# Splitting the second half of x before the first evictions of the value product

## The chip, the cores and the metric

The kernel runs on one core of one Trainium2 chip. The metric is the device time of one execution in microseconds (us), taken as the median of several runs. Everything below about the chip is read from one profiled execution.

## The reference

The kernel computes one layer of a decoder trunk for 1024 tokens of width 1024, in float32. Only the first lines matter here.

```python
h = x @ w_in                       # columns = [pool | q | k | v | forget-gate]
pool_out = pool_mixer(u, pool_w, pool_scale)
attn_out = forgetting_attention(q, k, v, f_logit)     # 8 heads, causal
x = layer_norm(alpha * x + concat(pool_out, attn_out) @ w_out)
x = layer_norm(alpha * x + relu(x @ w_mlp1)**2 @ w_mlp2)
```

The stage that the change touches is the part of `x @ w_in` that gives the values v and the forget-gate logits, 520 columns together.

## The kernel before

**Split products.** A float32 operand is held as a high part and a low part. `split(hi, lo, src)` makes them with one cast on ScalarE (hi, L71) and one subtraction on VectorE (lo, L72, which reads hi). A product of two such operands is three matmuls into the same PSUM bank: hi by hi (L83), hi by lo (L84), lo by hi (L85), in the helper `three`.

**The value product.** Tokens come in two halves of 512 (c = 0 and 1), each as four blocks of 512 KB that `load_x(c, kp)` loads into a staging slot (tag "Q") and splits into slots of tag "B", two k-tiles of 128 rows for each block. The weights `wvf` come in four blocks of 520 KB. For the first half eight PSUM banks, all that there are, are accumulated at once: 4 token tiles by 2 column halves (260 columns each), with the contraction index k outermost, so 8 x 8 x 3 = 192 matmuls. `vf_out` then evicts each bank: a ScalarE cast (L161), a VectorE subtraction (L162) and a small VectorE addition that takes the gate logits (L164). After that the second half runs bank by bank, again 192 matmuls. Its matmuls need two things: the splits of x for c = 1, and a bank that `vf_out` has released.

**Output weights.** Between the tiles of the second half, `split_output_weights(k)` splits five 512 KB blocks of `wout` (ScalarE cast L198, VectorE subtraction L199), and GpSimd stores both parts to DRAM (L201, ten stores of 512 KB). These blocks are loaded behind x on the SyncE queue (L194), and three 512 KB blocks of the next weights `wuqk` (L76, tag "S") follow them. What comes next on TensorE is the first pool projection, `pool_group`, with its own weights.

**Order of work.** The kernel is traced in the order of its source, and a planner then fixes the order of the instructions on each engine before the program runs: among those that it takes to be ready it prefers the one traced first, and slots of one tag are given out in the order in which they were asked for. So the order on an engine need not be the order of the source. On the chip each engine follows the order given and waits on semaphores. `tc.issue_after(ins)` adds for every instruction traced in its block an edge that places it behind `ins` on the engine of `ins`; instructions of other engines get none, and no semaphore is added.

Of the kernel before, what the change touches and what calls it, by code (L numbers as in the profile page):

```python
# [8 lines left out]
F32 = mybir.dt.float32  # L9
# [3 lines left out]
ALU = mybir.AluOpType  # L13
# [23 lines left out]
def trunk(ctx, tc, xT, xn, wuqk, wvf, bf, poolw, pscale, wout, g1, b1, w1, w2, g2, b2, out):  # L37
# [5 lines left out]
    nc = tc.nc  # L43
# [7 lines left out]
    def slot(tag, shape, dt=F32R):  # L51
        uid[0] += 1
        return sb.tile([P] + list(shape), dt, tag=tag, bufs=NBUF[tag], name=f"{tag}{uid[0]}")
# [9 lines left out]
    def bank(tag=None):  # L63
        uid[0] += 1
        if tag is None:
            tag = CYCLE[rr[0] % 8]
            rr[0] += 1
        return ps.tile([P, CH], F32, tag=tag, bufs=PBUF[tag], name=f"{tag}{uid[0]}")

    def split(hi, lo, src):  # L70
        nc.scalar.copy(hi, src)  # L71
        nc.vector.tensor_tensor(lo, src, hi.bitcast(F32), ALU.subtract)  # L72

    def load_w(src):
        st = slot("S", [KT, P], F32)
        nc.sync.dma_start(st, src)  # L76
        w = slot("B", [2, KT, P])
        split(w[:, 0], w[:, 1], st)
        return w[:, 0], w[:, 1]
# [35 lines left out]
    def load_x(c, kp):  # L115
        st = slot("Q", [2, CH], F32)
        x = slot("B", [2, 2, CH])
        if c or kp:
            nc.sync.dma_start(st, xT[c, kp])
        for k in range(2):  # L120
            t = x[:, k]
            xs[c, 2 * kp + k] = t
            first = c == kp == k == 0
            for i, r in enumerate((slice(0, 256), slice(256, CH)) if first else (slice(0, CH),)):
                if c == kp == 0:
                    (nc.scalar if first and i == 0 else nc.sync).dma_start(st[:, k, r], xT[c, kp, :, k, r])
                split(t[:, 0, r], t[:, 1, r], st[:, k, r])
                yield

    wv = []  # L130

    def load_wvf(kp):
        st = slot("S", [2, 2 * VW], F32)
        hi, lo = slot("A", [2, 2 * VW]), slot("A", [2, 2 * VW])
        wv.append((hi, lo))
        if kp:
            nc.sync.dma_start(st, wvf[kp])
        for k in range(2):
            if kp == 0:
                nc.sync.dma_start(st[:, k], wvf[kp, :, k])  # L140
            for c in [slice(0, VW), slice(VW, 2 * VW)] if kp == 0 and k == 0 else [slice(0, 2 * VW)]:
                split(hi[:, k, c], lo[:, k, c], st[:, k, c])
                yield
# [4 lines left out]
    def vf_mm(t, half, dst, k):  # L148
        x = xs[t // 4, k]
        tok = slice((t % 4) * P, (t % 4 + 1) * P)  # L150
        cols = slice(half * VW, (half + 1) * VW)
        w = wv[k // 2]
        three(dst, (x[:, 0, tok], x[:, 1, tok]), (w[0][:, k % 2, cols], w[1][:, k % 2, cols]), k == 0, k == KT - 1)

    def vf_out(t, half, src):
        if V[t] is None:
            v2 = slot("B", [2, NH, 2, HD])
            V[t - t % 2], V[t - t % 2 + 1] = v2[:, 0], v2[:, 1]
        vv = V[t][:, 4 * half : 4 * half + 4]
        sv = src[:, 0 : 4 * HD].rearrange("p (h d) -> p h d", h=4)  # L160
        nc.scalar.copy(vv[:, :, 0, :], sv)  # L161
        nc.vector.tensor_tensor(vv[:, :, 1, :], sv, vv[:, :, 0, :].bitcast(F32), ALU.subtract)  # L162
        hs = slice(4 * half, 4 * half + 4)
        nc.vector.tensor_tensor(z[:, t, hs], src[:, 4 * HD : VW], bf_sb[:, hs], ALU.add)  # L164


    acc0 = [tuple(bank()[:, 0:VW] for _ in range(2)) for t in range(4)]
# [5 lines left out]
    for kp in range(4):  # L173

        gw, gx = load_wvf(kp), load_x(0, kp)
        for g in (gw, gx, gw, gx, gw, gx):
            next(g, None)
    nc.sync.dma_start(bf_sb, bf)
    nc.sync.dma_start(ps_sb, pscale)
    for k in range(KT):  # L180
        for t in range(4):
            for half in range(2):
                vf_mm(t, half, acc0[t][half], k)
    for t in range(4):
        for half in range(2):
            vf_out(t, half, acc0[t][half])
    for kp in range(4):
        for _ in load_x(1, kp):
            pass

    raw = {}
    for k in range(ASIDE, KT):
# [10 lines left out]
    for t in range(4, NT):  # L203
        for half in range(2):
# [4 lines left out]
            k = ASIDE + 2 * (t - 4) + half  # L209
# [1049 lines left out]
```

## Time and profile before

| | |
|---|---|
| Median of 3 runs | 1039.18 us (1038.84 to 1039.32) |
| The profiled execution, its time | 1040.64 us |
| The profiled execution, its span from first to last instruction | 1038.9 us |
| Mean granted TensorE clock | 0.996 of full speed |
| TensorE busy | 1018.5 us, 98% of the span |
| VectorE / ScalarE / GpSimd busy | 756.6 / 513.6 / 155.0 us |

The span leaves out 1.74 us of the execution's own time that lie around it. The engines are named PE (TensorE matmul), PEld (its weight load), DVE (VectorE), ACT (ScalarE), POOL (GpSimd) and SP (SyncE); a q behind a name is the engine's queue that issues transfers.

### The profile page before, as it was taken

The numbers are of one execution on the slowest core, as the hardware profiler recorded it, in microseconds if no ns is written. First come the engines' busy times: TensorE is split into PE (matmuls) and PEld (weight loads), VectorE is DVE, ScalarE is ACT, GpSimd is POOL, SyncE is SP. The second block draws the span as 40 slices with busy tenths as digits, with TensorE's granted clock in tenths as the row PEclk, the third lists the DMA queues.
The fourth block names the chain that finished last, engine by engine and source line by source line (L and its number), as shares of the span: only waits on it lengthen the run. The fifth ranks groups of instructions, "written<-read, shape, count | busy, mean of one in ns | idle before, by whom it ended". The sixth has DMA issues, their size and how long they took to land.

```text
span 1038.9 us, 14121 instructions
## 1 busy us (share of the span) xinstructions
PE 1018.5 (98%) x4976; PEld 846.5 (81%) x4976; DVE 756.6 (73%) x1300; ACT 513.6 (49%) x823; POOL 155.0 (15%) x267
## 2 busy tenths in 40 slices
PE   9999999999989999999999999999999999999996
PEld 9988887888767888787888888888878888888884
DVE  4777678677767887989888778788885666565547
ACT  4523566666665332676666766768621211122152
POOL 0200112112100031112122122120100000000047
PEclk9999999999999999999999999999999999999998
DMA  9702311111584532139767567565999888878753
GB/s 359 273 28 82 111 65 32 36 47 54 173 281 140 185 122 99 61 125 353 275 229 276 224 253 273 217 265 184 346 316 321 283 258 283 275 222 269 242 186 121
DMA packets 113671, 206.30 MB, mean 199 GB/s; under 512 B 9592, under 2 KB 78008, under 8 KB 113600
## 3 DMA queue, kind: packets, MB, share of 16 engines
q1 hardware_dynamic: 94608, 137.63, 40.5%
q0 software_dynamic: 18560, 67.12, 16.7%
q8 instruction: 39, 0.64, 0.2%
q10 hardware_dynamic: 432, 0.66, 0.2%
q14 instruction: 32, 0.26, 0.1%
HBM read 132.42 MB, written 72.94 MB: 198 GB/s over the span
## 4 chain that ended last, share of the span: by engine, by line
PE 49%; issue 4%; DVE 3%; DMA 2%; POOL 1%; ACT 0%; DVEq 0%; POOLq 0%; SPq 0%
PE s L1060 15%; PE pv L1060 8%; PE s L727 8%; PE mm L727 6%; PE pt L727 6%; PE pv L727 4%; PE pt L1060 2%; PE mm L1060 2%; DMA S<-in_w_dram 2%; DVE B L72 1%; DMA hid_dram<-A 1%; POOL hid_dram L852 0%; POOL A L720 0%; DVE A L850 0%; DVE bns L573 0%
## 5 line engine op out<-in xcount | busy, mean ns | idle before, releaser
L71 ACT CAST B<-S 128x1024 fp32r<-128x1024 f32 (+1 forms) x78 | 67.7, 881 | 169.4 <-DMA S<-in_w_dram 67.5
L727 PE MATMUL s<-B,Q 128*128 128x512 f32 x492 | 116.4, 389 | 0.2 <-ACT B L71 0.2
L727 PEld LDWEIGHTS s<-B,Q 128*128 128x128 f32 x492 | 92.3, 188 | 19.8 <-ACT B L71 0.6
L72 DVE TENSOR_TENSOR B<-S,B 128x1024 fp32r<-128x1024 f32 (+1 forms) x78 | 78.0, 1008 | 34.0 <-ACT B L71 33.9
L1060 PE MATMUL s<-B,Q 128*128 128x512 f32 x402 | 98.2, 390 | 0.0
L1060 PEld LDWEIGHTS s<-B,Q 128*128 128x128 f32 x402 | 75.5, 188 | 16.2
L71 ACT CAST Q<-S 128x1024 fp32r<-128x1024 f32 x53 | 55.7, 1051 | 58.0 <-PE s L727 17.0
L852 POOL DMA_DIRECT2D hid_dram<-A x90 | 48.1, 537 | 221.5 <-ACT A L849 164.6
L1060 PE MATMUL s<-B,A 128*128 128x512 f32 x321 | 79.7, 393 | 0.0
L72 DVE TENSOR_TENSOR Q<-S,Q 128x1024 fp32r<-128x1024 f32 x53 | 65.6, 1238 | 15.3 <-ACT Q L71 14.8
L727 PE MATMUL pt<-B,Q 128*128 128x512 f32 x312 | 74.6, 389 | 0.0
L727 PE MATMUL mm<-B,Q 128*128 128x512 f32 x300 | 71.6, 389 | 0.0
L1060 PEld LDWEIGHTS s<-B,A 128*128 128x128 f32 x321 | 60.3, 188 | 13.5
L727 PEld LDWEIGHTS pt<-B,Q 128*128 128x128 f32 x312 | 58.5, 188 | 12.1
L727 PEld LDWEIGHTS mm<-B,Q 128*128 128x128 f32 x300 | 56.3, 188 | 11.7
L377 ACT ACTIVATE A<-A,nm 128x1024 f32<-128x1024 f32 (+7 forms) x64 | 49.7, 778 | 32.3 <-DVE nm L375 31.1
L416 PE MATMUL pv<-A,B 128*128 128x256 f32 x320 | 62.2, 295 | 2.7 <-DVE A L399 1.3
L416 PEld LDWEIGHTS pv<-A,B 128*128 128x128 f32 x320 | 51.0, 188 | 17.1 <-ACT A L398 6.9
L399 DVE TENSOR_TENSOR A<-pt,A 128x512 fp32r<-128x512 f32 (+1 forms) x80 | 49.6, 634 | 15.2 <-ACT A L398 14.4
L850 DVE TENSOR_TENSOR A<-A,A 128x1024 f32<-128x1024 f32 x45 | 53.6, 1219 | 0.0
L362 POOL TENSOR_TENSOR A<-A,maskb 128x128 f32<-128x128 f32 x48 | 23.5, 492 | 190.8 <-DVE nm L375 131.8
L398 ACT CAST A<-pt 128x512 fp32r<-128x512 f32 (+1 forms) x80 | 41.4, 542 | 19.3 <-PE pt L397 18.4
(427 smaller groups left out, 2341.7 us busy)
## 6 DMA issues: line engine op xcount, KB each, us to landing
hid_dram<-A POOLq DMA_DIRECT2D x105, 512.0 KB, 4.0
S<-in_w_dram SPq DMA_DIRECT2D x62, 512.0 KB
Q<-hid_dram SPq DMA_DIRECT2D x98, 256.0 KB
A<-hid_dram SPq DMA_DIRECT2D x82, 256.0 KB
S<-in_wuqk_dram SPq DMA_DIRECT2D x12, 512.0 KB
wo_dram<-Q POOLq DMA_DIRECT2D x10, 512.0 KB, 3.8
B<-wo_dram SPq DMA_DIRECT2D x10, 512.0 KB
Q<-hid_dram SPq DMA_DIRECT2D x39, 128.0 KB
```

The lines of the kernel that those rows point to most:

```text
L71: nc.scalar.copy(hi, src)
L72: nc.vector.tensor_tensor(lo, src, hi.bitcast(F32), ALU.subtract)
L362: nc.gpsimd.tensor_tensor(nb[:, qs], nb[:, qs], maskb, ALU.add)
L377: nc.scalar.activation(pt[:, :nk], pt[:, :nk], AF.Exp, bias=nm, scale=-1.0, accum_out=rsum[h][:, i : i + 1])
L398: nc.scalar.copy(tt[:, 0, ev], tp[:, ev])
L399: nc.vector.tensor_tensor(tt[:, 1, ev], tp[:, ev], tt[:, 0, ev].bitcast(F32), ALU.subtract)
L416: nc.tensor.matmul(ov, V[j][:, h].rearrange("p s d -> p (s d)"), tt[:, s, a:b], start=(j == 0 and s == 0), stop=(j == 2 * m + 1 and s == 1),)
L727: nc.tensor.matmul(dst, b[x][:, k], A[a][y][:, k], start=first and k == 0 and i == 0, stop=k == H - 1 and i == 2, skip_group_check=not first,)
L850: nc.vector.tensor_tensor(x, x, hi.bitcast(F32), ALU.subtract)
L852: nc.gpsimd.dma_start(hid_dram[self.u, :, i, AT[name] : AT[name] + 2 * CH], part.rearrange("p q n t -> p (q n t)"))
L1060: nc.tensor.matmul(dst, h[:, p_], w[q_], start=first and u == self.us[0] and j == 0, stop=u == self.us[-1] and j == 2, skip_group_check=no ...
```

## The change

`load_x` now hands out the two instructions of each split. The four blocks of the second token half are traced before the eight evictions, and the evictions are traced inside two `issue_after` blocks: on ScalarE they stand behind the last cast of x, on VectorE behind the last subtraction of x. The number of instructions, their shapes and the transfers stay as they were.

```diff
     def split(hi, lo, src):
-        nc.scalar.copy(hi, src)
-        nc.vector.tensor_tensor(lo, src, hi.bitcast(F32), ALU.subtract)
+        return nc.scalar.copy(hi, src).ins, nc.vector.tensor_tensor(lo, src, hi.bitcast(F32), ALU.subtract).ins
...
-                split(t[:, 0, r], t[:, 1, r], st[:, k, r])
-                yield
+                yield split(t[:, 0, r], t[:, 1, r], st[:, k, r])
...
-    for t in range(4):
-        for half in range(2):
-            vf_out(t, half, acc0[t][half])
     for kp in range(4):
-        for _ in load_x(1, kp):
+        for behind in load_x(1, kp):
             pass
+    with tc.issue_after(behind[0]), tc.issue_after(behind[1]):
+        for t in range(4):
+            for half in range(2):
+                vf_out(t, half, acc0[t][half])
```

## Rows read from the trace of the kernel before

**Rows 1.** The page's part 1: busy us, share of the span, instructions.
```profile
PE 1018.5 (98%) x4976; PEld 846.5 (81%) x4976; DVE 756.6 (73%) x1300; ACT 513.6 (49%) x823; POOL 155.0 (15%) x267
```
**Rows 2.** Waits on PE: who waited for whom, us in total, times, longest.
```profile
PE s L83 <- ACT B L71: 1.5, 1, 1.5
PE pv L416 <- DVE A L399: 1.3, 5, 0.3
```
**Rows 3.** Timeline of PE, 26 to 54 us: start, duration, instruction, idle before it.
```profile
26.21 0.28 PE L85 MATMUL mm<-A,B 128*128 128x260 f32 x1
...
29.09 0.28 PE L85 MATMUL mm<-A,B 128*128 128x260 f32 x1
30.86 0.39 PE L83 MATMUL s<-A,B 128*128 128x260 f32 x1 [1.48 <-ACT B L71]
31.08 0.28 PE L84 MATMUL s<-A,B 128*128 128x260 f32 x1
...
54.02 0.28 PE L85 MATMUL mm<-A,B 128*128 128x260 f32 x1
```
**Rows 4.** Timeline of ACT, 15 to 60 us (xN merges neighbours).
```profile
14.95 1.14 ACT L71 CAST B<-Q 128x512 fp32r<-128x512 f32 x2 [0.16 <-DMA Q<-in_xT_dram]
26.89 0.37 ACT L161 CAST B<-s 128x256 fp32r<-128x256 f32 x1 [10.79 <-PE s L85]
...
27.87 1.05 ACT L198 CAST Q<-Q 128x1024 fp32r<-128x1024 f32 x1
...
30.13 4.31 ACT L71 CAST B<-Q 128x512 fp32r<-128x512 f32 x8
...
46.65 2.00 ACT L71 CAST B<-S 128x1024 fp32r<-128x1024 f32 x2
```
**Rows 5.** Timeline of DVE, 15 to 60 us.
```profile
15.61 1.29 DVE L72 TENSOR_TENSOR B<-Q,B 128x512 fp32r<-128x512 f32 x2
...
27.29 0.42 DVE L162 TENSOR_TENSOR B<-s,B 128x256 fp32r<-128x256 f32 x1 [10.33 <-ACT B L161]
27.63 0.15 DVE L164 TENSOR_TENSOR z<-s,bf 128x4 f32<-128x4 f32 x1
...
28.95 1.22 DVE L199 TENSOR_TENSOR Q<-Q,Q 128x1024 f32<-128x1024 f32 x1 [0.36 <-ACT Q L198]
...
32.10 4.90 DVE L72 TENSOR_TENSOR B<-Q,B 128x512 fp32r<-128x512 f32 x8
```
**Rows 6.** Timeline of SP's queue, 0 to 60 us: issues of transfers.
```profile
8.80 3.88 SPq L119 DMA_DIRECT2D Q<-in_xT_dram  x4
...
17.84 31.48 SPq L76 DMA_DIRECT2D S<-in_wuqk_dram  x4
```
**Rows 7.** Windows of the first 30 us: busy by engine, PE clock, DMA share, GB/s.
```profile
0.00:7.20 7.20, 6.01 (x27) 6.00 (x28) 2.41 (x6) 3.14 (x6) 1.62 (x24) 1.00 0.70 234
7.20:16.00 8.80, 8.80 (x75) 8.80 (x74) 7.51 (x13) 7.43 (x13) 0.00 (x0) 1.00 1.02 403
16.00:27.00 11.00, 11.00 (x94) 11.00 (x93) 0.96 (x3) 0.21 (x2) 0.00 (x0) 1.00 1.03 409
...
29.00:30.00 1.00, 0.37 (x4) 0.17 (x2) 1.00 (x1) 1.00 (x5) 0.73 (x1) 1.00 0.18 70
```
**Rows 8.** Timeline of POOL, 15 to 60 us: the first store of output weights.
```profile
29.22 0.73 POOL L201 DMA_DIRECT2D wo_dram<-Q  x1 [27.03 <-ACT B L161]
```
**Rows 9.** Windows of the stages behind, columns as in rows 7.
```profile
54.00:130.00 76.00, 76.00 (x363) 62.65 (x362) 52.40 (x110) 31.25 (x54) 3.38 (x8) 1.00 0.24 76
130.00:250.00 120.00, 118.44 (x687) 98.72 (x686) 88.95 (x221) 75.55 (x165) 23.27 (x55) 1.00 0.15 45
250.00:430.00 180.00, 175.59 (x915) 143.26 (x913) 140.24 (x284) 84.97 (x168) 28.43 (x46) 1.00 0.46 151
430.00:520.00 90.00, 88.61 (x389) 72.86 (x389) 78.75 (x103) 64.80 (x86) 18.17 (x29) 1.00 0.61 228
520.00:1000.00 480.00, 479.55 (x2104) 394.50 (x2103) 340.41 (x456) 216.76 (x280) 48.03 (x80) 1.00 0.77 262
```

## The prediction

> **What bounds the kernel now.** I read the page's busy table first. PE is busy for 98% of the span [rows 1], so a change off PE can only give back what PE spends waiting. The list of PE's waits comes next, and its longest entry is in the stage of the change: one wait of 1.5 us of the value product for the cast of x on ACT [rows 2]. PE's timeline places it. The first half's last matmul starts at 29.09, the second half's first at 30.86, with 1.48 us idle, released by ACT's L71 [rows 3]. The timelines of ACT and DVE tell why that cast was late. ACT does nothing for 10.79 us up to 26.89, when the first eviction starts, and DVE nothing for 10.33 us up to 27.29; the eight casts of x stand behind the eight evictions and start only at 30.13, the subtractions at 32.10 [rows 4, 5]. Was x there earlier? Its four loads went out from 8.80 on [rows 6]. By the windows 234 GB/s x 7.2 us + 403 GB/s x 8.8 us = 5.23 MB had arrived by 16 us, and 409 GB/s follow [rows 7]. In the order of issue, x of the first half (2.10 MB), the value weights (2.13 MB) and x of the second half (2.10 MB) make 6.32 MB, so I estimate that the second half of x is complete at 16 + 1.09 / 0.409 = 18.7 us. The same count puts the five output-weight blocks (8.95 MB) at 25.1 us and the three next blocks (10.52 MB) at 28.9 us; that the rate drops to 70 GB/s in the window from 29 to 30 [rows 7] fits it. So the input lies ready for some 8 us, two engines idle, and the order on them makes PE wait.
>
> **The change part by part.**
>
> *The returned instructions of split* cost nothing: they are Python values, and no instruction comes or goes.
>
> *The splits move ahead.* ACT takes 4.31 us for the eight casts, 0.54 each [rows 4], and DVE 4.90 us for the eight subtractions, 0.61 each [rows 5]. ACT is free of the first half's work at 14.95 + 1.14 = 16.1, DVE at 15.61 + 1.29 = 16.9. The last block, two casts, lands at 18.7 by the estimate: ACT ends at 18.7 + 2 x 0.54 = 19.8, DVE one cast and two subtractions after the landing and no earlier than 16.9 + 4.9 = 21.8. Both lie inside the idle stretch, whose cover is PE's own work on the first half (11.00 of 11.00 us busy from 16 to 27, [rows 7]). Without that cover they would cost the stall that they cost now, 1.65 us as worked out below.
>
> *The evictions move behind.* They can't start before 26.89 anyway, since they wait for PE's last matmul of the bank [rows 4]. From 21.8 to 26.89 there are 5 us of slack. The waiting instruction is then an eviction at the same place in time as now, and behind it on ACT and DVE stand the other evictions, the output-weight splits and later the splits of the next weights. The first bank is free when DVE has done L162 and L164: 27.63 + 0.15 = 27.8 us [rows 5], against PE's need at 29.09 + 0.12 = 29.2. The second half runs bank by bank once all of x is split, 24 matmuls or 2.9 us for each bank, while DVE frees one about every 0.41 us; the later banks are not waited for.
>
> *What slips ahead of the evictions?* One output-weight cast (1.05 us on ACT, 1.22 us on DVE) already ran between evictions at 27.87 [rows 4, 5]; the planner could now put some ahead of the first. All five would take DVE from 21.8 to 27.9 and free the first bank at 28.5, still before 29.2. The next weights' casts (46.65, [rows 4]) ask for a B slot behind those of the second half's values and are needed by PE at 54 only; ACT's cast and DVE's subtraction end some four us before that, and both move with the evictions of the second half.
>
> *The gain.* PE's pace is (29.09 - 26.21) / 24 = 0.120 us a matmul [rows 3]. From 29.09 to the second half's last start at 54.02 are 192 steps: 24.93 us, where the pace asks for 23.04. The excess is 1.89 us: 30.86 - 29.09 - 0.12 = 1.65 at the stall, 0.10 at the step after it (31.08), the other 0.14 in small slips while the order still follows the late splits. The lower end is 1.65, the upper 1.89; I take 1.8, near the upper end, since the slips come from the same lateness. If something else holds PE at 29.2, the lower end is nothing or less (rivals below).
>
> *What passes it on.* From 54 to 130 us PE is busy for 76.00 of 76.00 us, from 520 to 1000 for 479.55 of 480 [rows 9]; the moved pieces are PE's own, and the waits in between (1.56, 4.41 and 1.39 us of idle from 130 to 520) belong to chains of ACT and DVE that start from PE's results and move with them. The DMA share there is 0.15 to 0.77, so no stream sets a fixed time. The clock is 1.00 in all the windows from the stall to 1000 us, so the shorter stall can't buy any.
>
> *The sum.* The profiled execution took 1040.64 us, 1038.9 of span and 1.74 around it; less 1.8 that is 1038.84. It lies 1.46 above the median shown, so for the median I expect 1039.18 - 1.8 = 1037.4 us. A run here can tell about 0.2%, 2.08 us, from no change; the forecast is just inside that.
>
> **The rivals.**
>
> *A: x lands late, and the wait changes its name.* My landing time is counted, not seen. If the transfers in flight share the rate instead of coming in turn, the last block of x lands at most at 28.9. Then DVE's last subtraction ends at 28.9 + 0.6 + 1.2 = 30.7, the first bank is free at 31.2, and PE starts at 31.3 instead of 30.86: 0.44 lost, some 0.24 of slips regained, 1039.4 us. The change pays nothing from a landing at about 28.5 on. For it speaks that no row shows the landing; against it that the first half's blocks, in the same queue, were split as they came, the last at 14.95 to 16.1, close behind their 4.2 MB. The Trainium skill ("TensorE: Matmul & The Clock Gate", on the engine queue depths) says that ACT and DVE keep strict order, so an eviction can't overtake a split that waits; the 10.8 idle us of ACT agree, and by that rule alone this rival has the same 1039.4 us.
>
> *B: slower, by the stores of the output weights.* If the planner puts all five output-weight splits ahead of the evictions, POOL's stores, first seen at 29.22 [rows 8], start near 21.4 us, while 1.5 MB of the five loads are outstanding. Were the rate of 409 GB/s halved by them, the last block would land at 21.4 + 1.5 / 0.2045 = 28.8; cast, subtraction and eviction (1.05 + 1.22 + 0.57) free the first bank at 31.6, and PE starts 0.8 us later than now: with the slips regained 0.55 slower, 1039.7 us. It decides from a first bank free later than 30.8. Against it: at 27.87 the planner took one such cast and gave the next place to an eviction [rows 4]. That queues share the engines is what the Trainium skill says ("Trainium Kernel Development and Optimization", Key Constraints: transfers of the SP, ACT and POOL queues run on the same 16 engines and interleave). No stretch in rows 7 has loads and stores together, so nothing read here shows the halving; with that rule and this order the time is 1039.7, without the sharing 1037.4.
>
> *C: no effect at the end.* The gain is made and some later wait on a fixed time eats it: 1039.2 us. The full PE from 54 to 130 speaks against it [rows 9].
>
> *D: the plan behind changes.* Pieces that the planner sees earlier may be ordered otherwise through the whole program. PE idles 7.8 us between 54 and 1000 [rows 9]; winning one more of them gives 1036.4, losing two 1039.4, more than that a slower kernel.
>
> **How the numbers follow.** The forecast has 0.60, within 1036.8 to 1037.8. A 0.08 and B 0.08, C 0.06. D upward (over 0.2% faster) 0.14, D downward, over 0.2% slower, 0.04. About three tenths of the forecast's weight, 0.18, lie below 1037.1 us, because the excess reaches 1.89 and small gains of order may join it. So faster is 0.14 + 0.18 = 0.32, slower 0.04, same the remaining 0.64. The range reaches from 1036.2 (most of D upward) to 1039.4 (A and C); outside are B, D downward and the tail of D upward, some 0.17.
>
> **What would show it.** Right: eight L71 casts of x on ACT between 16 and 21 us and the subtractions by 22; the first L161 still at about 26.9; PE's gap behind 29.09 gone, and the last matmul of the second half near 52.2 instead of 54.02. Wrong: L161 later than 29, released by a transfer or behind L198 or L199 (A, B); a gap of PE with L162 or L164 as its releaser; an early second half but an unmoved end (C); new waits in the attention or the MLP (D).

## The result and the profile after

| | before | after |
|---|---|---|
| Median | 1038.97 us (22 runs, 1037.8 to 1043.1) | 1037.11 us (22 runs, 1035.8 to 1038.81) |
| Ratio | | 0.9982, 95% interval 0.9975 to 0.9988 |
| Profiled execution: time, span | 1040.64, 1038.9 us | 1038.5, 1036.7 us |

The change makes the kernel faster by 1.86 us between the medians, 0.18%; by the interval it is 1.2 to 2.6 us. The forecast was a gain of 1.8 us and 1037.4 us, from the earlier median of 1039.18; 1037.11 lies within its 1036.8 to 1037.8.

In the lines of after the split helper has line 71 for both its instructions, the product L82 to L84 and the eviction L159, L160, L162. The list of PE's waits no longer holds the value product, whose 1.5 us headed it before; the other entries differ by up to 0.4 us.

```profile
PE pv L415 <- DVE A L398: 1.3, 5, 0.3
PE mm L169 <- DVE Q L167: 1.2, 1, 1.2
PE pt L396 <- ACT row L434: 1.1, 1, 1.1
```

The timeline of PE around the end of the first half, against [rows 3]:

```profile
28.51 0.28 PE L84 MATMUL mm<-A,B 128*128 128x260 f32 x1
28.63 0.28 PE L82 MATMUL s<-A,B 128*128 128x260 f32 x1
28.75 0.28 PE L83 MATMUL s<-A,B 128*128 128x260 f32 x1
28.87 0.28 PE L84 MATMUL s<-A,B 128*128 128x260 f32 x1
28.99 0.28 PE L82 MATMUL s<-A,B 128*128 128x260 f32 x1
...
51.56 0.28 PE L84 MATMUL mm<-A,B 128*128 128x260 f32 x1
```

The second half starts one step of 0.12 us behind the first. I call the time from the first half's last matmul to the second half's last (192 steps) the stage: it was 54.02 - 29.09 = 24.93 us and is 51.56 - 28.51 = 23.05. That is 1.88 us, measured on PE itself.

PE's own order in the stage changed too. In the kernel before, the second half did not run bank by bank, as the source has it: the planner let PE do the two matmuls that need no low part of x (L83, L84) in each of the eight banks in turn, and the first L85 came only as the 17th matmul. The same timeline before, from the third matmul on:

```profile
31.20 0.28 PE L83 MATMUL pt<-A,B 128*128 128x260 f32 x1
31.32 0.28 PE L84 MATMUL pt<-A,B 128*128 128x260 f32 x1
...
31.68 0.28 PE L83 MATMUL mm<-A,B 128*128 128x260 f32 x1
...
32.88 0.34 PE L85 MATMUL s<-A,B 128*128 128x260 f32 x1
```

There PE asks for a new bank every 0.24 us. In the kernel after it finishes all 24 matmuls of a bank first and asks for a new one every 2.9 us. Experiment 3 shows what that is worth.

The timeline of ACT, against [rows 4]:

```profile
14.96 1.15 ACT L71 CAST B<-Q 128x512 fp32r<-128x512 f32 x2 [0.18 <-DMA Q<-in_xT_dram]
16.33 1.14 ACT L71 CAST B<-Q 128x512 fp32r<-128x512 f32 x2 [0.22 <-DMA Q<-in_xT_dram]
18.27 3.70 ACT L71 CAST B<-Q 128x512 fp32r<-128x512 f32 x6 [0.79 <-DMA Q<-in_xT_dram]
26.30 0.37 ACT L159 CAST B<-s 128x256 fp32r<-128x256 f32 x1 [4.33 <-PE s L84]
...
27.28 1.05 ACT L197 CAST Q<-Q 128x1024 fp32r<-128x1024 f32 x1
```

The timeline of DVE, against [rows 5]:

```profile
16.99 1.29 DVE L71 TENSOR_TENSOR B<-Q,B 128x512 fp32r<-128x512 f32 x2
18.92 3.86 DVE L71 TENSOR_TENSOR B<-Q,B 128x512 fp32r<-128x512 f32 x6 [0.64 <-ACT B L71]
26.71 0.42 DVE L160 TENSOR_TENSOR B<-s,B 128x256 fp32r<-128x256 f32 x1 [3.93 <-ACT B L159]
27.05 0.15 DVE L162 TENSOR_TENSOR z<-s,bf 128x4 f32<-128x4 f32 x1
...
29.51 0.42 DVE L160 TENSOR_TENSOR B<-mm,B 128x256 fp32r<-128x256 f32 x1
29.84 0.15 DVE L162 TENSOR_TENSOR z<-mm,bf 128x4 f32<-128x4 f32 x1
```

The eight casts now run as x lands, with a DMA as the releaser of the first two pairs, and end at 21.97; the subtractions end at 22.78. Then both engines wait again, 4.33 and 3.93 us, for PE's last matmul of the first bank, as before. That wait is what is left of the cover.

The two profiles differ by 2.2 us of span, and 0.58 of that is not the change. The first half ends at 28.51 instead of 29.09 because PE's matmuls fell from 0.42 to 0.28 us at 5.96 us in this execution and at 7.24 in the one of before; nothing before 16 us was changed. Behind the stage the order of the instructions on all five engines is the same in both programs. The lead of 2.46 us at the stage's end arrives as 2.2; a wait for `row` in the attention takes 1.1 instead of 0.8 us, and one near the end 0.8 instead of 0.4.

### The profile page after: what moved, and what is told of

It reads as the page before. It is cut to its first block, busy times and chain, and to the rows that moved or that the text cites. A ratio compares the mean times of both kernels' runs of the same rounds, so it can differ in the third digit from the quotient of the medians.

```text
span 1036.7 us, 14123 instructions
## 1 busy us (share of the span) xinstructions
PE 1017.7 (98%) x4976; PEld 845.6 (82%) x4976; DVE 757.3 (73%) x1300; ACT 514.4 (50%) x823; POOL 155.3 (15%) x267
## 4 chain that ended last, share of the span: by engine, by line
PE 49%; issue 4%; DVE 3%; DMA 2%; POOL 1%; SPq 0%; ACT 0%; DVEq 0%; POOLq 0%
PE s L1059 15%; PE pv L1059 8%; PE s L726 8%; PE mm L726 6%; PE pt L726 6%; PE pv L726 4%; PE pt L1059 2%; PE mm L1059 2%; DMA S<-in_w_dram 2%; DMA hid_dram<-A 1%; DVE B L71 1%; POOL hid_dram L851 0%; POOL A L719 0%; DVE A L849 0%; SPq L1038 0%
## 5 line engine op out<-in xcount | busy, mean ns | idle before, releaser
L726 PEld LDWEIGHTS s<-B,Q 128*128 128x128 f32 x492 | 92.3, 188 | 19.8 <-ACT B L71 0.6
```

Of the source, the lines that this page charges most:

```text
L726: nc.tensor.matmul(dst, b[x][:, k], A[a][y][:, k], start=first and k == 0 and i == 0, stop=k == H - 1 and i == 2, skip_group_check=not first,)
```

## The experiments

All ratios are to the kernel before on the same chip, with 95% intervals. The edits are shown against the kernel after. Where an order is said to be the same, the traces have it the same instruction for instruction.

**1. Without the edges.** The trace order is kept, the `issue_after` blocks go.

```diff
-    with tc.issue_after(behind[0]), tc.issue_after(behind[1]):
-        for t in range(4):
-            for half in range(2):
-                vf_out(t, half, acc0[t][half])
+    for t in range(4):
+        for half in range(2):
+            vf_out(t, half, acc0[t][half])
```

> The changed kernel without the two issue_after blocks; only the tracing order of the x splits and the evictions is changed. Theory (the position of the x splits in the trace does it, the edges add nothing): the stage from the last matmul of the first half to the last of the second takes 23.05 us as in the changed kernel (24.93 before), and the time is 0.9982 of before within about 0.001. Rival (the edges are needed): evictions come ahead of some splits again, the stage takes up to 24.9 us and the ratio is 1.000.

Measured: 1037.29 us, 0.9978 (0.9969 to 0.9988), stage 51.25 - 28.20 = 23.05 us, on PE's timeline:

```profile
28.20 0.28 PE L84 MATMUL mm<-A,B 128*128 128x260 f32 x1
28.32 0.28 PE L82 MATMUL s<-A,B 128*128 128x260 f32 x1
...
51.25 0.28 PE L84 MATMUL mm<-A,B 128*128 128x260 f32 x1
```

The order on all five engines is that of the changed kernel. So the edges do nothing here; tracing the loads and splits of x ahead of the evictions does it. The difference between 0.9978 and 0.9982 is what two runs of one program can show. Why the planner left the splits behind the evictions when these were traced first is not settled by the runs.

**2. One block ahead.**

```diff
-    for kp in range(4):
-        for behind in load_x(1, kp):
-            pass
+    for behind in load_x(1, 0):
+        pass
     with tc.issue_after(behind[0]), tc.issue_after(behind[1]):
...
+    for kp in range(1, 4):
+        for _ in load_x(1, kp):
+            pass
```

> Only the first of the four x blocks (two k-tiles) is split ahead of the evictions, the other three behind them. Theory (PE waited only for the first splits; six more k-tiles are split while PE works on the first two in all eight banks, 48 matmuls or 5.8 us): gap behind the first half below 0.2 us, the stage 23.1 to 23.3 us, ratio 0.998 to 0.9985. Rival (all eight splits must be out of the way, since the rest queue behind the evictions until 29.9 on ScalarE and 32 on VectorE): a wait of 0.5 us or more for L71 inside the second half and a stage above 23.6 us, ratio 0.9987 to 1.000.

Measured: 1036.99 us, 0.9982 (0.9972 to 0.9991), stage 51.79 - 28.58 = 23.21 us. No wait of PE is listed in the stage. PE's order is neither that of before nor that of after, and not the 48 matmuls on the first two k-tiles that the theory counted on: twelve matmuls in two banks come first, and the 14th waits 0.09 us, too short for the list, for the cast of the third k-tile.

```profile
28.58 0.28 PE L84 MATMUL mm<-A,B 128*128 128x260 f32 x1
28.70 0.28 PE L82 MATMUL s<-A,B 128*128 128x260 f32 x1
...
51.79 0.28 PE L84 MATMUL mm<-A,B 128*128 128x260 f32 x1
```

In that order two k-tiles ahead are enough for PE to go on while the other six are split (ACT 29.61 to 32.88, DVE 31.58 to 35.27). With them 1.72 of the 1.88 us are there; the last 0.16 go in the two long steps at that cast, 30.34 and 30.57.

**3. The casts alone.** ACT's half of the change only.

```diff
-        nc.vector.tensor_tensor(z[:, t, hs], src[:, 4 * HD : VW], bf_sb[:, hs], ALU.add)
+        return nc.vector.tensor_tensor(z[:, t, hs], src[:, 4 * HD : VW], bf_sb[:, hs], ALU.add).ins
...
+    held = []
     for kp in range(4):
-        for behind in load_x(1, kp):
-            pass
-    with tc.issue_after(behind[0]), tc.issue_after(behind[1]):
-        for t in range(4):
-            for half in range(2):
-                vf_out(t, half, acc0[t][half])
+        st, x = slot("Q", [2, CH], F32), slot("B", [2, 2, CH])
+        nc.sync.dma_start(st, xT[1, kp])
+        for k in range(2):
+            xs[1, 2 * kp + k] = x[:, k]
+            nc.scalar.copy(x[:, k, 0], st[:, k])
+            held.append((x[:, k], st[:, k]))
+    for t in range(4):
+        for half in range(2):
+            behind = vf_out(t, half, acc0[t][half])
+    with tc.issue_after(behind):
+        for x, st in held:
+            nc.vector.tensor_tensor(x[:, 1], st, x[:, 0].bitcast(F32), ALU.subtract)
```

> Only ScalarE's half of the change: the eight casts of x stand ahead of the evictions, the eight subtractions are held behind the last eviction on VectorE, where they stood before; TensorE and VectorE have the order of before. Theory (both halves are needed: VectorE is free of the evictions only at 32.1 us, and TensorE can do 16 matmuls without a low part): the gap behind the first half goes, and TensorE waits about 1.5 us for the first subtraction instead; stage 24.5 to 24.9 us, ratio 0.9995 to 1.000. Rival (TensorE waited for the cast alone, as its releaser in the profile says): stage 23.1 to 23.3 us, ratio 0.998 to 0.9985.

Measured: 1038.79 us, 0.9995 (0.9986 to 1.0003), stage 53.47 - 28.54 = 24.93 us, exactly that of before. The order on PE and DVE is that of before. PE starts at 28.66 and stops again after six matmuls; timelines of PE and, for the fourth bank, of DVE:

```profile
30.17 0.36 PE L82 MATMUL mm<-A,B 128*128 128x260 f32 x1 [0.63 <-DVE z L162]
...
31.77 0.36 PE L82 MATMUL mm<-A,B 128*128 128x260 f32 x1
31.97 0.28 PE L83 MATMUL mm<-A,B 128*128 128x260 f32 x1
32.28 0.39 PE L84 MATMUL s<-A,B 128*128 128x260 f32 x1
```
```profile
29.54 0.42 DVE L160 TENSOR_TENSOR B<-mm,B 128x256 fp32r<-128x256 f32 x1
29.87 0.15 DVE L162 TENSOR_TENSOR z<-mm,bf 128x4 f32<-128x4 f32 x1
```

In this order PE does only two matmuls in each bank until a low part is there. It first waits for the fourth bank, whose eviction on DVE stands behind an output-weight subtraction of 1.22 us, then goes at DVE's 0.40 us for a bank, 0.20 for a matmul, and last meets the first subtraction of x, which starts at 31.54. The size came as expected, by another path: most of the new wait is for banks (0.79 us at 30.17 and 0.08 at each of the next nine steps), not for low parts. The profile of before named ACT's cast as the releaser; taking that wait away alone gave nothing, because DVE's queue was as late for PE's order. The banks themselves come no earlier in the changed kernel: DVE frees the fourth at 29.84 + 0.15 = 29.99 us there and at 30.02 here. There PE asks for it only behind 72 matmuls. So three orders go together in the gain: the casts on ACT, the subtractions on DVE, and one of PE that asks for the banks later, which the planner chose with them. Both splits ahead with PE in the order of before was not run; since the banks come at the same times, I estimate that most of the 1.51 us of waits for banks would stay.

**4. The output weights ahead as well (rival B).** The loads of `wout` and the helper move up too; the helper returns its two instructions.

```diff
...
+    for k in range(ASIDE, KT):
+        behind = split_output_weights(k)
     with tc.issue_after(behind[0]), tc.issue_after(behind[1]):
         for t in range(4):
...
-            k = ASIDE + 2 * (t - 4) + half
-            if k < KT:
-                split_output_weights(k)
```

> The changed kernel with all five output-weight splits also ahead of the evictions on ScalarE and VectorE (rival B of the prediction, forced). Blocks in the changed kernel were ready for their casts some 1.5 to 2 us later than counted, so the fifth block is ready near 27.0 us if the stores take nothing from the loads: then its cast ends at 28.1, its subtraction at 29.3, the first bank is free at 29.9 and TensorE waits 1.2 us (stage 24.3 us, ratio 0.9993). If the stores of the first blocks take half of the rate, the block is ready near 30.7 us, the first bank free at 33.5, TensorE waits 4.9 us: stage 28 us, ratio 1.003. Rival (these splits fit under the first half too): no wait, stage 23.1 us, ratio 0.998.

Measured: 1038.62 us, 0.9998 (0.9989 to 1.0006), stage 52.97 - 29.03 = 23.94 us. Timelines of ACT, DVE, POOL and PE, one line of each or two:

```profile
25.83 1.06 ACT L193 CAST Q<-Q 128x1024 fp32r<-128x1024 f32 x1 [0.21 <-DMA Q<-in_wout_dram]
27.11 1.05 ACT L193 CAST Q<-Q 128x1024 fp32r<-128x1024 f32 x1 [0.22 <-DMA Q<-in_wout_dram]
```
```profile
23.11 6.31 DVE L193 TENSOR_TENSOR Q<-Q,Q 128x1024 f32<-128x1024 f32 x5 [0.50 <-ACT Q L193]
29.34 0.42 DVE L160 TENSOR_TENSOR B<-s,B 128x256 fp32r<-128x256 f32 x1
```
```profile
23.38 0.73 POOL L195 DMA_DIRECT2D wo_dram<-Q  x1 [21.19 <-ACT Q L193]
```
```profile
29.97 0.36 PE L82 MATMUL s<-A,B 128*128 128x260 f32 x1 [0.67 <-DVE z L162]
```

The fifth block is ready for its cast at 27.11, as the count without halving had it, and the blocks keep coming every 1.27 us while the first stores have long been issued. The list of DMA queues (kind, packets, MB, share of 16 engines) shows why, first for 22 to 24 us and then for 28 to 30; q1 is SP's loads, q0 POOL's stores:

```profile
q1 hardware_dynamic: 224, 0.81, 101.5%
...
q1 hardware_dynamic: 116, 0.43, 52.6%
q0 software_dynamic: 116, 0.41, 50.8%
```

No packet of a store shows before 27 us, though the first was issued at 23.38; once they flow, loads and stores have about half of the engines' time each. The fall of the loads hits the next weights, which have time. PE waits 0.82 us over a step for the first bank, since DVE's five subtractions end at 29.42. Against after, the stage loses 0.89 us. The whole time can't confirm that size: from 0.9982 to 0.9998 are 1.7 us, and each ratio is known to about 1 us.

**5. x lands late (rival A).** n transfers that nothing uses go out ahead of x; PE's order is that of after; ACT and DVE differ from it only in the place of the output-weight splits.

```diff
+    for i in range(n):
+        pad = dr.tile([P, D], F32, name=f"pad{i}")
+        nc.sync.dma_start(pad, wout[i % KT])
     for kp in range(4):
         for behind in load_x(1, kp):
```

> The changed kernel with four extra 512 KB transfers (DRAM to DRAM, used by nothing) issued ahead of the x loads of the second half, so that x lands later (rival A of the prediction, forced). In the runs so far the last block is ready near 20.5 us; the last subtraction ends 1.8 us and the first bank is free 2.4 us after that, while TensorE asks for it at 28.6: the change should lose nothing until the last block is ready at 26.2. Theory 1 (a transfer takes 512 KB at 410 GB/s, 1.28 us each): delay 5.1 us, ready at 25.6, no wait, stage 23.05 to 23.2 us, ratio 0.998 to 0.9985. Theory 2 (it counts twice, read and write): delay 10.2 us, ready at 30.7, TensorE waits 4.5 us, stage 27.5 us, ratio 1.0025.

> As with four extra transfers, with six. Theory 1: delay 7.7 us, ready at 28.2, wait 2.0 us, stage 25.0 us, ratio 1.000. Theory 2: delay 15.4 us, ready at 35.9, wait 9.7 us, stage 32.7 us, ratio 1.0075. If waits are absorbed later in the program, the stage is as long but the ratio stays nearer 0.998.

> As with four extra transfers, with eight. Theory 1: delay 10.2 us, ready at 30.7, wait 4.5 us, stage 27.5 us, ratio 1.0025. Theory 2: delay 20.5 us, ready at 41, wait 14.8 us, stage 37.8 us, ratio 1.0125. What the stage loses should arrive at the end of the program microsecond for microsecond; if the end moves less, something behind absorbs it (rival C).

| n | first cast of x (16.33 us in after) | last subtraction ends | PE starts the second half | stage | ratio |
|---|---|---|---|---|---|
| 4 | 22.09 | 27.88 | 28.43 | 51.43 - 28.29 = 23.14 | 0.999 (0.998 to 1.0) |
| 6 | 25.19 | 31.24 | 31.79 | 54.80 - 29.00 = 25.80 | 1.0018 (1.0009 to 1.0027) |
| 8 | 29.29 | 35.09 | 35.64 | 61.37 - 28.32 = 33.05 | 1.0073 (1.0058 to 1.0088) |

The end of the last subtraction is the sum of the start and length of DVE's rows; for six transfers they are

```profile
25.84 1.29 DVE L71 TENSOR_TENSOR B<-Q,B 128x512 fp32r<-128x512 f32 x2 [9.14 <-ACT B L71]
27.40 3.84 DVE L71 TENSOR_TENSOR B<-Q,B 128x512 fp32r<-128x512 f32 x6 [0.27 <-ACT B L71]
31.16 0.42 DVE L160 TENSOR_TENSOR B<-s,B 128x256 fp32r<-128x256 f32 x1
31.50 0.15 DVE L162 TENSOR_TENSOR z<-s,bf 128x4 f32<-128x4 f32 x1
```

and PE's answer is

```profile
29.00 0.28 PE L84 MATMUL mm<-A,B 128*128 128x260 f32 x1
31.79 0.36 PE L82 MATMUL s<-A,B 128*128 128x260 f32 x1 [2.52 <-DVE z L162]
```

PE starts 0.55 us after the last subtraction in all three. With four transfers that is just in time: the five us of slack are used up and cost 0.09 us. Beyond it each microsecond is paid. Eight come out 5.5 us longer than theory 1 had it: PE waits 7.2 us and not 4.5, and it loses another 2.8 by its clock (last section). A transfer delays x by 1.4 to 1.6 us, nearer to theory 1 (1.28) than to theory 2. For eight transfers the stage is 8.12 us longer than before, 0.78%, and the ratio is 0.73% (0.58 to 0.88): no later part of the program is seen to absorb it. For six the stage gives +0.08% and the ratio +0.18%; its interval ends just above the stage's figure, and what makes the difference is open.

## Why the prediction held, point by point

**What was late.** The reading of the busy table, the waits and the three timelines was right: the input lay ready, two engines idled, and their order made PE wait. Experiment 2 shows that the first two k-tiles ahead bring all but 0.16 us of it, in an order of PE that the planner fitted to them.

**The landing of x.** The count of bytes put the last block at 18.7 us, and the casts' end at 19.8. The first block was ready at 16.33 and the second at 18.27, against 14.8 and 16.1 by the same count, so blocks could be used 1.5 to 2.2 us after the bytes are counted in; the casts ended at 21.97, the subtractions at 22.78 instead of 21.8. The error of 2 us went into slack, which experiment 5 measured at some five us.

**The evictions.** They did not move: 26.30 against 26.89, which is the 0.58 us of the earlier end of the first half. The output-weight cast stayed in fourth place. That the later banks are not waited for rested on PE running bank by bank once x is split. No row of before showed that order, since PE there went through the banks two matmuls at a time; the planner did give it, and experiment 3 shows that in the other order the fourth bank and those behind it are waited for. This step came out right without having been priced.

**The gain.** The bounds were 1.65 and 1.89 with 1.8 taken; the stage gives 1.88, the upper end. The slips of 0.24 that I had put down to late splits did go; 0.16 us of such slips return in experiment 2, where six k-tiles are late. The step that reads a stall from one releaser was lucky in one respect. I had costed the change as if ACT's cast were the wait; experiment 3 shows that with DVE and PE in the order of before all of it comes back, 1.51 us as waits for banks and most of the rest at the first low part. The casts have no gain of their own in that order.

**What passes it on.** The gain arrives, 1.86 us between medians against 1.88 in the stage, and losses do too (eight transfers). Rival C is out.

**Rival A** has its mechanism right, and its tipping point is shown: PE restarts 0.55 us after the last subtraction, where I had 0.6. (Its landing of 28.5 us, from which the change pays nothing, leaves out the slips regained; with them its own sum gives 28.7.) That evictions can't overtake a split whose data is late, as the Trainium skill says of ACT's and DVE's strict order ("TensorE: Matmul & The Clock Gate", on the engine queue depths), agrees with experiment 5: with six transfers ACT's first eviction starts at 30.34, right behind the last cast of x, though the last matmul of its bank started at 26.46. **Rival B** had one step wrong. Loads and stores do share the engines, about half each (52.6% and 50.8%), which agrees with the Trainium skill ("Trainium Kernel Development and Optimization", Key Constraints), but no packet of a store moves before 27 us, when the five blocks are nearly in. Forced, the order costs 0.89 us of the stage and not the 2.3 us by which B's 1039.7 stands above the forecast; the whole time does not tell the two apart. **Rival D** did not happen: the order behind the stage is unchanged.

## What to carry to other kernels

An engine that idles ahead of an eviction is a place for any work whose input is already there, as long as the eviction behind it still frees its bank before the next user asks. The slack is the idle time ahead of the eviction (3.9 us on DVE here) and the time from the free bank to that user (27.20 to 28.63), and it is paid one for one when it is used up. Before one releaser of a stall is removed, look at where the other queues stand at that time, and in which order the waiting engine asks for what they release: here the cast alone bought nothing. And a count of bytes gives when a block has moved, not when an engine may use it; add what the rows of the same queue show, here 1.5 to 2.2 us.

## What the hardware showed that was not expected

With eight transfers PE idled for 7.04 us, and it came back at half its clock. The windows (PE, PEld, DVE, ACT, POOL busy, PE clock, DMA share, GB/s):

```profile
28.00:30.00 2.00, 0.60 (x6) 0.39 (x4) 0.06 (x1) 0.71 (x2) 0.00 (x0) 1.00 0.97 356
30.00:32.00 2.00, 0.00 (x0) 0.00 (x0) 2.00 (x4) 1.70 (x4) 0.00 (x0) 0.87 1.03 420
32.00:34.00 2.00, 0.00 (x0) 0.00 (x0) 2.00 (x4) 1.86 (x4) 0.00 (x0) 0.50 1.03 422
...
36.00:38.00 2.00, 2.00 (x11) 2.00 (x11) 2.00 (x11) 2.00 (x4) 0.28 (x1) 0.50 1.03 410
...
42.00:44.00 2.00, 2.00 (x19) 2.00 (x18) 2.00 (x4) 1.48 (x2) 0.47 (x1) 1.00 1.02 414
```

The granted clock is 1.00 (2.4 GHz) up to the idle time, falls to 0.50 (1.2 GHz) in it, stays there while PE is busy again from 35.64, and is 1.00 from 42 us on; the matmuls take 0.42 us and follow each other every 0.217 us until 41.6 instead of every 0.12. That makes most of the 2.8 us between the stage's loss of 10.0 us and the wait of 7.2. The idle 2.52 us with six transfers cost no clock: its matmuls follow each other every 0.12 us from 31.99 on. So the stall of 1.48 us that the change removed had no such price, and the forced one of 7.04 us has.

Stores issued by POOL at 23.38 us showed no packet until 27, while SP's queue held loads; the ten took a median of 11.3 us to land, against 3.8 in the kernel before. Whether the queued loads or POOL's own preparation kept them was not tried.
